# A planner's instruction times, steps of one half of the partitions, and one product moved from GpSimd to VectorE

## The chip, the cores and the metric

The kernel runs on one core of a Trainium2 chip. TensorE multiplies matrices (PE in the profile; PEld is its weight load), VectorE (DVE), ScalarE (ACT) and GpSimd (POOL) work on elements, SyncE (SP) issues transfers. The metric is the device time of one execution in microseconds; the median of three runs before the change is 2248.6 us (2247.82 to 2249.54).

## The reference

One decoder layer over 2048 tokens of width 1024, all in float32. The normalised input is projected by one wide matrix; the pieces feed three branches, whose outputs are gated, projected, merged and added to the input.

```python
h = rms_norm(x, norm_g[l])
p = h @ w_in[l]
y_a = rwkv7_mix(...) * jax.nn.silu(z_a)
y_b = sliding_window_sink_attn(...) * jax.nn.silu(z_b)
y_c = memory_cross_attn(...) * jax.nn.silu(z_c)
merged = gates[:, :, 0] * (y_a @ w_proj_a[l]) + gates[:, :, 1] * (y_b @ w_proj_b[l]) + gates[:, :, 2] * (y_c @ w_proj_c[l])
x = x + merged @ w_out[l]
```

Branch A is a recurrence over time with 8 heads of width 64. Its keys are normalised per head: `kk = kk / max(norm(kk), 1e-12)`. The change touches the place where those norms enter.

## The kernel before

**Tiling.** Tokens are worked in four blocks of 512 (`sb`), channels by 128 partitions. Large matmuls are 128x128 by 128x512 and come in threes: each float32 operand is split into a high and a low part, and `gemm3` (L457, L458, L459) adds high times high, high times low, low times high in one PSUM tile. `wblock` brings such weights: in the first block from the inputs, with the split on ScalarE (L439) and VectorE (L440) and a copy of it kept in DRAM; later from that copy.

**Streams.** In a block two streams are interleaved. `stream_r` is branch A, two groups of two head pairs. A pair occupies 128 partitions: the even head the lower 64, the odd head the upper 64 (`EV`, `OD`). `rwkv_prep` makes the operands of a pair. Within it, `dk` holds one over the squared norms (L722), and L723 and L724 fill the tile `AB` [128, 8 chunks, 128] on GpSimd: the right half with the mask `gmask`, the left half with `gmask` times `dk`, both broadcast. L726 to L737 and L742 make the operands Q and BK from the keys, decays and receptance on VectorE; 32 matmuls (L753) into four PSUM banks multiply them; L760 and L761 take the results out of PSUM, multiplying by `AB` and by `gmask`, for each bank first one half of the partitions, then the other. L770 transposes BK on TensorE; L766 and L771 copy on ScalarE. `rwkv_inverse` solves small triangular systems, mostly on VectorE (L803 to L805). `rwkv_chain` walks over the 8 chunks: two bursts of small matmuls on the state Z (L866, L867), W (L869), two more (L874, and L859 of the chunk before), a product with `dk` (L878), L881, and L882 for the next state; L872 prepares a scaled state on ScalarE. The small steps of the chain come for the even and the odd head in turn. `stream_f` has cross attention (`cross_head`), window attention (`swa_kv`, `swa_pair`), the merges of branches C and B and the gates of A. At the end of a block come the merge of A and the output projection (L1172 to L1174, L1179).

**Order.** The program is first written down as a list of instructions. `steps` turns each into a `Step` with what it reads and writes, those that it must follow, a rank (its place in the list, with shifts: steps outside TensorE that read PSUM move ahead by 600, the inverse's back by 500), and a cost by engine. `busy` is how long its engine is taken, `dur` how long until its result is there. Two steps that read the same PSUM tile are kept in the order of the list. `lay_out` then plays the program through with these costs: a clock for each engine, the time from which each step is ready, the buffers as they come free. Whenever an engine is free it takes, of the steps ready by then, the one of lowest rank; TensorE, once in a small tile of its array, stays with steps of that tile while it finds any. `order` makes the resulting sequence of every engine binding. So the costs never change what is computed, only in which order each engine does it.

Of the kernel before, what the change touches and what calls it, by code (L numbers as in the profile page):

```python
# [14 lines left out]
ALU = mybir.AluOpType  # L15
# [12 lines left out]
C = 64  # L28
NC_ = TB // C
# [26 lines left out]
class Step:  # L56


    def __init__(self, ins, masks):
        self.ins, self.eng = ins, NAMES[ins.engine]  # L60
        self.reads, self.writes = ([self.region(a.bass_ap, masks) for a in aps if getattr(a, "bass_ap", None) is not None]
                                   for aps in (ins.ins, ins.outs))
        self.reads, self.writes = ([r for r in l if r] for l in (self.reads, self.writes))
        self.before, self.after, self.opens, self.group, self.end = set(), [], [], [], None
        self.lat = LAT[self.eng]
        if self.eng == "PE" and not any(r[0].startswith(("Z_", "W_", "R_")) or r[0] in ("Z", "W", "R") for r in self.reads):
            self.lat = 600
        self.bytes = 512 * self.n((self.writes + self.reads)[0]) if self.is_dma() else 0
        getattr(self, "cost_" + ("SP" if self.bytes else self.eng))()

# [25 lines left out]
    def cost_PE(self):  # L96
        out, mov, w = self.writes[0], *self.reads[:2]
        n = self.n(out)
        self.tile = tuple(128 if r[3][0][1] > 64 else 64 if r[3][0][1] > 32 else 32 for r in (mov, out))
        self.dense = mov[5] == F32R  # L100
        if self.dense:
            self.busy = 14 + 0.424 * n
        elif self.ins.is_transpose:
            self.busy = 108 if self.tile[0] == 128 else 55
        elif self.tile[1] == 128:
            self.busy = 223 + max(0, n - 128) * 1.7 if self.tile[0] == 128 else 62 + max(0, n - 64) * 0.8
        else:
            self.busy = 32 if self.tile[1] == 32 else max(58, 0.86 * n)
        self.dur = max(270, self.busy + 160)

    def cost_ACT(self):
        r = self.reads[0]
        self.dur = (170 if r[4] else 206) + 0.83 * self.n(r) + 90 * (len(self.reads) - 1 + len(self.writes) - 1)
        self.busy = self.dur - (85 if len(self.writes) > 1 else 38 if r[4] else -12)
        self.table = {AF.Sin: 1, AF.Exp: 2, AF.Tanh: 2}.get(self.ins.func, 0)

    def cost_DVE(self):
        r, two = self.reads[0] if self.reads else self.writes[0], sum(self.n(x) > 1 for x in self.reads) > 1
        slow = two or r[4] or type(self.ins).__name__ not in ("InstTensorScalarPtr", "InstTensorCopy", "InstMemset")
        self.dur = 155 + (1.05 if slow else 0.53) * self.n(r) + 30 * (len(self.reads) - 1)  # L120
        self.busy = max(100, self.dur - 85)
        if two and r[4] and self.n(r) <= 128:
            self.busy = self.dur + 20

    def cost_POOL(self):
        n = self.n(self.writes[0])
# [54 lines left out]
def lay_out(tc, todo):  # L181

    metas = {tag: meta.bufs for p in tc.info.pools if p.space != bass.MemoryType.DRAM for tag, meta in p.tag_meta.items()}
    source = {t.name: t.source_name for t in tc.info.tiles}
    tags = {tag: Tag(b) for tag, b in metas.items()}
    users, opened = {}, set()
    for s in todo:
        for name in {r[0] for r in s.reads + s.writes}:
            users.setdefault(name, []).append(s)
        for r in s.writes:  # L190
            if source[r[0]] in tags and r[0] not in opened:
                opened.add(r[0])
                s.opens.append(r[0])
                tags[source[r[0]]].queue.append(r[0])
    left = {name: len(u) for name, u in users.items()}
    heads = {tag: 0 for tag in tags}
    clock = {e: 0.0 for e in NAMES.values()}
    ready, parked = {e: {} for e in clock}, set()
    orders = {e: [] for e in clock}
    missing = {s: len(s.before) for s in todo}  # L200

    def seen_by(s, b):

        if b.eng == s.eng:
            return 0 if s.eng == "PE" else b.end + 30
        return b.end + s.lat

    def room(s):

        at, taken = 0.0, {}  # L210
        for name in s.opens + [n for g in s.group for n in g.opens]:
            tag = source[name]
            t, i = tags[tag], taken.get(tag, 0)
            if t.queue[heads[tag] + i] != name or len(t.free) <= i:
                return None
            taken[tag] = i + 1
            old = t.free[i]
            if old:
                at = max([at] + [seen_by(s, b) for b in last[old].values()])
        return at  # L220

    def offer(s):
        at = room(s)
        if at is None:
            parked.add(s)
            ready[s.eng].pop(s, None)
        else:
            parked.discard(s)
            ready[s.eng][s] = max([at] + [seen_by(s, b) for b in s.before])

    last = {name: {} for name in users}
    for s in todo:
        if not missing[s]:
            offer(s)
    tile, fp32, wires, table = (128, 128), False, 0, 2
    for _ in todo:
        best = None
        for e, rs in ready.items():
            if rs:
                at = max(clock[e], min(rs.values()))  # L240
                if best is None or at < best[0]:
                    best = at, e
        at, e = best
        can = [s for s, t in ready[e].items() if t <= at]
        s = min(can, key=lambda s: s.rank)
        if e == "PE":
            if tile != (128, 128) and s.tile != tile:
                s = min(can, key=lambda s: (s.tile != tile, s.dense, s.rank))
            if s.tile != tile:
                at += 95  # L250
            clock[e] = at + s.busy
            if s.dense and fp32:
                clock[e] += 95
            elif s.tile != tile and s.tile[1] < 128:
                clock[e] += 49
            tile, fp32 = s.tile, not s.dense
        else:
            if e == "ACT" and not s.bytes and s.table and s.table != table:
                at, table = at + 1280, s.table
            clock[e] = at + s.busy  # L260
        s.end = at + s.dur
        if s.bytes:
            wires = s.end = max(wires, s.end) + s.bytes / 330
        del ready[e][s]
        orders[e].append(s)
        again = set()
        for name in s.opens:
            tag = source[name]
            tags[tag].free.pop(0)
            heads[tag] += 1  # L270
            again.add(tag)
        for name in {r[0] for r in s.reads + s.writes}:
            if e not in last[name] or last[name][e].end < s.end:
                last[name][e] = s
            left[name] -= 1
            if not left[name] and source[name] in tags:
                tags[source[name]].free.append(name)
                again.add(source[name])
        for a in s.after:
            missing[a] -= 1  # L280
            if not missing[a]:
                offer(a)
        if again:
            for a in [a for rs in (parked, *ready.values()) for a in rs if any(source[n] in again for g in [a, *a.group] for n in g.opens)]:
                offer(a)
    return orders
# [11 lines left out]
def build(tc, A, nsb=4):  # L298
    nc = tc.nc
    es = ExitStack()  # L300
    V, S, G, PE = nc.vector, nc.scalar, nc.gpsimd, nc.tensor
# [82 lines left out]
    gmask = cp.tile([128, 128], BF16, name="gmask")  # L384
# [286 lines left out]
    def rwkv_prep(p, i, Z, dk, Nc, sb, hT, lwla, group):  # L671
        def big(name):

            if not i:
                return rp.tile([128, NC_, 128], F32, name=name)
            t = wp.tile([128, NC_, 128], F32, name="whl")
            G.memset(t[:, 0, 0:1], 0.0)
            return t

        QE, QO, AB, BK = (big(n) for n in ("QE", "QO", "AB", "BK"))  # L680
# [40 lines left out]
                    V.tensor_scalar(own[h, :, o], sums[at, :, e], 1e-24, None, op0=ALU.max)  # L721
        V.reciprocal(dk[:, i], dk[:, i])  # L722
        G.tensor_copy(AB[:, :, C:], gmask[:, C:].unsqueeze(1).to_broadcast([128, NC_, C]))  # L723
        G.tensor_tensor(AB[:, :, :C], gmask[:, :C].unsqueeze(1).to_broadcast([128, NC_, C]), dk[:, i].unsqueeze(2).to_broadcast([128, NC_, C]), op=ALU.mult)  # L724
        kkh = tmp()
        V.tensor_scalar(kkh, k, dcol("hk_k", p), None, op0=ALU.mult)  # L726
        for Q, h in ((QE, EV), (QO, OD)):
# [12 lines left out]
        r = shift(rpj, B_R + p, pcol("mu_r", p), dcol("omu_r", p), sb, "rr_")  # L740
# [6 lines left out]
        two = ((QE, EV, OD), (QO, OD, EV))  # L747
# [631 lines left out]
```

## Time and profile before

| | |
|---|---|
| median of three runs | 2248.6 us |
| profiled execution | 2250.41 us |
| its span, first to last instruction | 2248.6 us |
| ScalarE steps / VectorE steps / GpSimd steps | 2024 / 3951 / 209 |
| VectorE's inverse, L803 + L804 + L805 | 113.3 + 104.4 + 102.9 us |
| weight split, L439 and L440 | 111.1 and 123.3 us |
| read and written in HBM | 333.24 and 94.90 MB |

A row of the groups gives line, engine, operation, output and inputs, shape, count, then busy us, mean ns of one, and the idle time of the engine before them with what ended it. Matmuls overlap in the pipe, and their ends are modelled, so their spacing is read from the starts in the timeline and not from their durations. A row of the timeline is start, length, engine, line, operation; "x4" is four merged ones.

### The profile page before, as it was taken

How to read it: one execution, taken by the hardware profiler on the slowest of the kernel's cores; microseconds unless marked ns; L12 is line 12 of the kernel's file. 1: busy time of each engine (PE TensorE's matmuls, PEld its weight loads, DVE VectorE, ACT ScalarE, POOL GpSimd, SP SyncE). 2: the span in 40 equal slices, each digit the busy share in tenths (PEclk: the TensorE clock that was granted, in tenths of full speed). 3: DMA queues.
4: the chain of work that ended last, by engine and by line, in shares of the span. 5: the costliest groups of instructions: out<-in, count | busy, mean ns of one | idle time of the engine just before them, and what ended most of it. 6: DMA issues, size and time to landing. Idle time of an engine off the chain costs nothing.

```text
span 2248.6 us, 36877 instructions
## 1 busy us (share of the span) xinstructions
PE 2219.2 (99%) x13706; PEld 1804.8 (80%) x13706; DVE 1531.7 (68%) x3951; ACT 926.1 (41%) x2024; POOL 149.7 (7%) x209
## 2 busy tenths in 40 slices
PE   8999999999999999999999999999999999999999
PEld 7887778778888778878888878787878887787887
DVE  6799699775479777953437957985245895896312
ACT  6664565545253354423214345442223435434210
POOL 2000010000000011000000001000000001100000
PEclk9999999999999999999999999999999999999999
DMA  6767556679944444447774434445675444343655
GB/s 215 271 232 245 191 188 220 221 269 353 324 146 160 134 141 150 147 165 235 239 239 136 164 122 150 148 135 195 229 250 199 157 142 160 115 148 132 206 191 193
DMA packets 146226, 430.55 MB, mean 191 GB/s; under 512 B 16640, under 2 KB 21120, under 8 KB 146048
## 3 DMA queue, kind: packets, MB, share of 16 engines
q1 hardware_dynamic: 129920, 398.83, 52.4%
q10 hardware_dynamic: 16128, 29.37, 4.0%
q8 instruction: 109, 1.79, 0.3%
q14 instruction: 69, 0.57, 0.1%
HBM read 333.24 MB, written 94.90 MB: 190 GB/s over the span
## 4 chain that ended last, share of the span: by engine, by line
PE 73%; DVE 18%; ACT 3%; DMA 2%; issue 2%; POOL 1%; SPq 0%; ACTq 0%; DVEq 0%; POOLq 0%
PE mm L457 18%; PE mm L459 18%; PE mm L458 17%; DVE ibc L803 2%; DVE ibc L804 1%; PE rw L881 1%; DVE Yi L805 1%; PE mm L1172 1%; PE mm L1173 1%; PE mm L1174 1%; ACT g L1102 1%; PE oo L1003 1%; DVE whl L440 1%; PE rw L866 1%; PE rw L874 1%
## 5 line engine op out<-in xcount | busy, mean ns | idle before, releaser
L457 PE MATMUL mm<-hH,whl 128*128 128x512 f32 x1888 | 750.0, 397 | 1.5 <-DVE gt L928 1.5
L459 PE MATMUL mm<-hH,whl 128*128 128x512 f32 x1888 | 748.3, 396 | 0.0
L458 PE MATMUL mm<-hL,whl 128*128 128x512 f32 x1888 | 748.0, 396 | 0.0
L457 PEld LDWEIGHTS mm<-hH,whl 128*128 128x128 f32 x1888 | 354.8, 188 | 72.7 <-DVE gt L928 1.9
L459 PEld LDWEIGHTS mm<-hH,whl 128*128 128x128 f32 x1888 | 354.8, 188 | 69.7
L458 PEld LDWEIGHTS mm<-hL,whl 128*128 128x128 f32 x1888 | 355.0, 188 | 67.8 <-issue 0.5
L439 ACT ACTIVATE whl<-raw 128x512 fp32r<-128x512 f32 x178 | 111.1, 629 | 144.8 <-PE mm L459 89.7
L440 DVE TENSOR_TENSOR whl<-raw,whl 128x512 fp32r<-128x512 f32 x178 | 123.3, 696 | 52.3 <-ACT whl L439 51.5
L457 PE MATMUL mm<-yh,whl 128*128 128x512 f32 x384 | 151.5, 395 | 1.4 <-DVE gt L1155 0.8
L459 PE MATMUL mm<-yh,whl 128*128 128x512 f32 x384 | 150.8, 393 | 0.0
L458 PE MATMUL mm<-yl,whl 128*128 128x512 f32 x384 | 150.7, 392 | 0.0
L872 ACT ACTIVATE SP<-Z,Pl 64x64 f32<-64x64 f32 x256 | 88.3, 345 | 112.7 <-DVE Z L882 109.2
L803 DVE STREAM_SHUFFLE ibc<-Nc 128x496 f32<-128x496 f32 (+30 forms) x248 | 113.3, 472 | 0.1
L1155 DVE SCALAR_TENSOR_TENSOR g<-g,mm 128x512 f32<-128x512 f32 x32 | 21.8, 680 | 128.6 <-PE mm L459 128.5
L804 DVE TENSOR_TENSOR ibc<-ibc,Yi 128x496 f32<-128x496 f32 (+30 forms) x248 | 104.4, 421 | 4.0
L805 DVE TENSOR_TENSOR Yi<-Yi,ibc 128x496 f32<-128x496 f32 (+30 forms) x248 | 102.9, 415 | 0.9
L1140 ACT ACTIVATE gt<-mm 128x512 f32<-128x512 f32 x64 | 38.0, 594 | 145.3 <-PE mm L459 145.1
L882 DVE SCALAR_TENSOR_TENSOR Z<-rw,Pl,SP 64x64 f32<-64x64 f32 x224 | 63.5, 283 | 50.0 <-PE rw L881 46.4
L457 PEld LDWEIGHTS mm<-yh,whl 128*128 128x128 f32 x384 | 72.1, 188 | 17.3 <-DVE g L1155 1.5
L459 PEld LDWEIGHTS mm<-yh,whl 128*128 128x128 f32 x384 | 72.1, 188 | 14.9
L458 PEld LDWEIGHTS mm<-yl,whl 128*128 128x128 f32 x384 | 72.1, 188 | 14.1
L1102 ACT ACTIVATE g<-g,mxs,st 128x256 f32<-128x256 f32 (+1 forms) x128 | 74.5, 584 | 18.8 <-DVE mxs L1095 18.6
(1812 smaller groups left out, 3786.7 us busy)
## 6 DMA issues: line engine op xcount, KB each, us to landing
whl<-k SPq DMA_DIRECT2D x486, 512.0 KB, 3.4
k<-whl SPq DMA_DIRECT2D x162, 512.0 KB, 4.3
raw<-in_w_in SPq DMA_DIRECT2D x118, 256.0 KB, 3.3
g<-in_x ACTq DMA_DIRECT2D x32, 256.0 KB, 4.4
out<-g ACTq DMA_DIRECT2D x32, 256.0 KB, 4.9
raw<-in_w_proj SPq DMA_DIRECT2D x24, 256.0 KB, 3.1
rt<-in_x ACTq DMA_DIRECT2D x24, 256.0 KB, 5.2
rt<-in_xt ACTq DMA_DIRECT2D x24, 256.0 KB, 5.8
```

The source lines that it names most:

```text
L439: S.activation(w[:, 0], raw, AF.Copy)
L440: V.tensor_tensor(w[:, 1], raw, w[:, 0].bitcast(F32), op=ALU.subtract)
L457: PE.matmul(out, lh, rh, start=i == 0, stop=False)
L458: PE.matmul(out, lh, rl, start=False, stop=False)
L459: PE.matmul(out, ll, rh, start=False, stop=i == n - 1)
L803: V.stream_shuffle(bc[:, :, :w], N_[:, :, s + 1:], [s] * 32)
L804: V.tensor_tensor(bc[:, :, :w], bc[:, :, :w], Y[:, :, s:s + 1].to_broadcast([128, n, w]), op=ALU.mult)
L805: V.tensor_tensor(Y[:, :, s + 1:], Y[:, :, s + 1:], bc[:, :, :w], op=ALU.add)
L872: S.activation(SP[h, i], Z[h, i, e, c], AF.Copy, scale=g[4][h, c:c + 1])
L882: upds = [V.scalar_tensor_tensor(Sst[h, g[0]] if c == NC_ - 1 else Z[h, i, e, c + 1], pS[h, i, e], g[4][h, c:c + 1], SP[h, i], op0=ALU.mul ...
L1102: S.activation(prs[b][:, i, m0:], prs[b][:, i, m0:], AF.Exp, scale=r2[:, b, i:i + 1], bias=mx[:, b, i:i + 1], accum_out=mx[:, b, 2 + i:3 + i])
L1140: S.activation(t, gp, AF.Tanh, scale=0.5)
```

## The change

Three edits. First, the formulas for `busy` and `dur` on TensorE, ScalarE and VectorE get other constants and cases: a scan has a fixed 1225 ns, shuffles and transposes 40 ns more, small operands are charged at 60 ns, a ScalarE step takes its engine for 97 ns less than its duration (15 with an accumulator). On TensorE a change of the tile delays the result by 97 ns and holds the engine 205 ns longer on the way back to large matmuls, 150 to other full tiles, 140 into small ones; the charge of 95 ns for a large matmul after a full-tile float32 one is gone.

Second, each step notes in `rows` the partition at which its output starts, and the highest at which an input starts. On VectorE and ScalarE the planner adds 20 to the rank of a step whose `rows` differ from those of the engine's last, and 105 ns to its start. Full-height steps and those of the lower half both start at 0, so they count as alike.

Third, the product of mask and norms (L724 before) goes from GpSimd to VectorE; the operands are the same. The term added to `seen_by` is zero for every engine.

```diff
+        outs = [a.bass_ap for l in (ins.outs, ins.ins) for a in l if getattr(a, "bass_ap", None) is not None]
+        rows = [a.offset // math.prod(list(a.tensor.shape)[1:]) for a in outs[:1] + [a.bass_ap for a in ins.ins if getattr(a, "bass_ap", None) is not None]]
+        self.rows = rows[0], max(rows)
...
-            self.busy = 14 + 0.424 * n
+            self.busy = 15 + 0.4167 * n
         elif self.ins.is_transpose:
-            self.busy = 108 if self.tile[0] == 128 else 55
+            self.busy = 112 if self.tile[0] == 128 else 55
         elif self.tile[1] == 128:
-            self.busy = 223 + max(0, n - 128) * 1.7 if self.tile[0] == 128 else 62 + max(0, n - 64) * 0.8
+            self.busy = 221 + max(0, n - 128) * 1.64 if self.tile[0] == 128 else 66 + max(0, n - 64) * 0.75
...
-        self.dur = (170 if r[4] else 206) + 0.83 * self.n(r) + 90 * (len(self.reads) - 1 + len(self.writes) - 1)
-        self.busy = self.dur - (85 if len(self.writes) > 1 else 38 if r[4] else -12)
+        self.dur = (170 if r[4] else 206) + 0.83 * self.n(r) + 90 * (len(self.reads) - 1)
+        self.busy = self.dur - (15 if len(self.writes) > 1 else 97)
...
-        self.dur = 155 + (1.05 if slow else 0.53) * self.n(r) + 30 * (len(self.reads) - 1)
-        self.busy = max(100, self.dur - 85)
-        if two and r[4] and self.n(r) <= 128:
-            self.busy = self.dur + 20
+        self.dur = 152 + (1.042 if slow else 0.52) * self.n(r) + 60 * (len(self.reads) - max(wide, 1))
+        if "Scan" in kind:
+            self.dur = 1225
+        elif kind in ("InstStreamShuffle", "InstStreamTranspose"):
+            self.dur += 40
+        self.busy = max(70, self.dur - 83)
...
-        s = min(can, key=lambda s: s.rank)
+        s = min(can, key=lambda s: s.rank + 20 * (e in ("DVE", "ACT") and s.rows != rows[e]))
...
+            clock[e] = at + s.busy
             if s.tile != tile:
-                at += 95
-            clock[e] = at + s.busy
-            if s.dense and fp32:
-                clock[e] += 95
-            elif s.tile != tile and s.tile[1] < 128:
-                clock[e] += 49
-            tile, fp32 = s.tile, not s.dense
+                at += 97
+                clock[e] += 205 if s.dense else 150 if s.tile == (128, 128) else 140
+            tile = s.tile
...
+            if s.rows != rows[e] and e in ("DVE", "ACT") and not s.bytes:
+                at += 105
+                rows[e] = s.rows
...
-        G.tensor_tensor(AB[:, :, :C], gmask[:, :C].unsqueeze(1).to_broadcast([128, NC_, C]), dk[:, i].unsqueeze(2).to_broadcast([128, NC_, C]), op=ALU.mult)
+        V.tensor_tensor(AB[:, :, :C], gmask[:, :C].unsqueeze(1).to_broadcast([128, NC_, C]), dk[:, i].unsqueeze(2).to_broadcast([128, NC_, C]), op=ALU.mult)
```

More of the change, by code (lines that the diff above doesn't have):

```diff
@@ L101, in cost_PE @@
         if self.dense:
-            self.busy = 14 + 0.424 * n
+            self.busy = 15 + 0.4167 * n
         elif self.ins.is_transpose:
-            self.busy = 108 if self.tile[0] == 128 else 55
+            self.busy = 112 if self.tile[0] == 128 else 55
         elif self.tile[1] == 128:
-            self.busy = 223 + max(0, n - 128) * 1.7 if self.tile[0] == 128 else 62 + max(0, n - 64) * 0.8
+            self.busy = 221 + max(0, n - 128) * 1.64 if self.tile[0] == 128 else 66 + max(0, n - 64) * 0.75
         else:
-            self.busy = 32 if self.tile[1] == 32 else max(58, 0.86 * n)
+            self.busy = 32 if self.tile[1] == 32 else max(60, 0.88 * n)
         self.dur = max(270, self.busy + 160)
@@ L112, in cost_ACT @@
         r = self.reads[0]
-        self.dur = (170 if r[4] else 206) + 0.83 * self.n(r) + 90 * (len(self.reads) - 1 + len(self.writes) - 1)
-        self.busy = self.dur - (85 if len(self.writes) > 1 else 38 if r[4] else -12)
+        self.dur = (170 if r[4] else 206) + 0.83 * self.n(r) + 90 * (len(self.reads) - 1)
+        self.busy = self.dur - (15 if len(self.writes) > 1 else 97)
         self.table = {AF.Sin: 1, AF.Exp: 2, AF.Tanh: 2}.get(self.ins.func, 0)
     def cost_DVE(self):
-        r, two = self.reads[0] if self.reads else self.writes[0], sum(self.n(x) > 1 for x in self.reads) > 1
-        slow = two or r[4] or type(self.ins).__name__ not in ("InstTensorScalarPtr", "InstTensorCopy", "InstMemset")
-        self.dur = 155 + (1.05 if slow else 0.53) * self.n(r) + 30 * (len(self.reads) - 1)
-        self.busy = max(100, self.dur - 85)
-        if two and r[4] and self.n(r) <= 128:
-            self.busy = self.dur + 20
+        r, wide = self.reads[0] if self.reads else self.writes[0], sum(self.n(x) > 1 for x in self.reads)
+        kind = type(self.ins).__name__
+        slow = wide > 1 or r[4] or kind not in ("InstTensorScalarPtr", "InstTensorCopy", "InstMemset")
+        self.dur = 152 + (1.042 if slow else 0.52) * self.n(r) + 60 * (len(self.reads) - max(wide, 1))
[4 more added lines that the diff above has]
+        self.busy = max(70, self.dur - 83)
     def cost_POOL(self):
@@ L205, in seen_by @@
             return 0 if s.eng == "PE" else b.end + 30
-        return b.end + s.lat
+        return b.end + s.lat + (0 if s.eng == "PE" else 0)
     def room(s):
@@ L234, in lay_out @@
             offer(s)
-    tile, fp32, wires, table = (128, 128), False, 0, 2
+    tile, wires, table = (128, 128), 0, 2
+    rows = {e: (0, 0) for e in clock}
     for _ in todo:
```

## The prediction

> **What bounds the kernel now.** I read the page's busy times first, then the busy time by stretches of the span, then the chain of waits of TensorE alone, and last the timeline around its waits.
>
> ```profile
> span 2248.6 us, 36877 instructions
> PE 2219.2 (99%) x13706; PEld 1804.8 (80%) x13706; DVE 1531.7 (68%) x3951; ACT 926.1 (41%) x2024; POOL 149.7 (7%) x209
> ```
>
> TensorE is busy for all but 29.4 us of 2248.6. Nothing in the change removes a matmul, so there are two places to win or lose: those 29.4 us, and time inside the busy figure that is not matmul work. The stretches show where the idle time lies (columns: stretch, length, busy us of PE, weight loads, DVE, ACT, POOL, clock, DMA share, GB/s).
>
> ```profile
> 0.00:25.00 25.00, 18.49 (x76) 15.66 (x77) 15.98 (x52) 13.03 (x30) 5.21 (x17) 0.80 0.70 226
> 25.00:500.00 475.00, 465.26 (x3090) 377.40 (x3090) 399.41 (x1004) 271.42 (x586) 43.00 (x55) 1.00 0.66 228
> 500.00:1025.00 525.00, 522.32 (x3271) 424.73 (x3270) 372.83 (x967) 220.69 (x482) 34.80 (x47) 1.00 0.56 192
> 1025.00:1087.00 62.00, 62.00 (x275) 51.35 (x274) 16.01 (x29) 16.96 (x34) 1.21 (x2) 1.00 0.68 227
> 1087.00:2181.00 1094.00, 1087.21 (x6721) 883.08 (x6719) 706.07 (x1869) 398.96 (x887) 65.46 (x88) 1.00 0.52 172
> 2181.00:2249.00 68.00, 63.97 (x283) 52.64 (x281) 21.42 (x32) 5.06 (x8) 0.00 (x0) 1.00 0.57 192
> ```
>
> Idle is 6.5 us in the first 25 (inputs arriving) and 4.0 at the end (last adds and stores, minus 0.4 of rounding of the window). Neither is a matter of order alone. Between lie 9.7 in the first block, 2.7, 0.0 and 6.8: 19.2 us. That is all that a better order can take out of idle time. The fourth row matters for the rivals: for 62 us before a block's last merge TensorE has work that waits for nobody, so the recurrent chain may end that much later at no cost. The waits behind the 19.2 us, from 25 us on (who waited, for whom, sum, times, longest):
>
> ```profile
> PE rw L866 <- DVE Z L882: 2.3, 4, 1.4
> PE rw L770 <- DVE QE L761: 2.1, 3, 0.7
> PE rw L753 <- DVE whl L737: 1.8, 1, 1.8
> PE mm L457 <- DVE gt L928: 1.5, 1, 1.5
> PE rw L770 <- DVE whl L761: 1.3, 3, 0.5
> PE rw L881 <- DVE Z L878: 1.3, 4, 0.4
> PE oo L1128 <- ACT g L1120: 1.0, 3, 0.4
> PE rw L785 <- DVE carry L661: 1.0, 3, 0.4
> PE rw L753 <- DVE QO L742: 0.8, 1, 0.8
> ```
>
> Nearly all end with VectorE, though VectorE is busy only 68%. The order on each engine is fixed when the program is built, by a planner that picks a step once it believes its inputs are there. With other matmuls in plenty, such a wait means that the planner had the VectorE step earlier, or TensorE later, than the chip did. So the question is which durations it had wrong, and whether the change mends those.
>
> **The change part by part.** *Product of mask and norms, GpSimd to VectorE.* 16 steps, two per group of two pairs.
>
> ```profile
> L724 POOL TENSOR_TENSOR AB<-gmask,dk 128x512 f32<-128x512 bf16 x8 | 11.5, 1436 | 52.7 <-DVE dk L722 52.7
> L724 POOL TENSOR_TENSOR whl<-gmask,dk 128x512 f32<-128x512 bf16 x8 | 10.9, 1358 | 185.2 <-DVE dk L722 185.2
> L732 DVE TENSOR_TENSOR BK<-rt x16: 674/690/1532, 68.5 to 1921.2; 64x512 f32<-64x512 f32 x16
> L732 DVE TENSOR_TENSOR whl<-rt x16: 629/686/1445, 117.8 to 1963.8; 64x512 f32<-64x512 f32 x16
> 826.14 0.64 DVE L735 TENSOR_TENSOR rk__8671<-rk__8671,rt 128x512 f32<-128x512 f32 x1
> 826.30 1.38 POOL L724 TENSOR_TENSOR AB<-gmask,dk 128x512 f32<-128x512 bf16 x1 [1.77 <-DVE dk L722]
> 826.69 1.53 DVE L732 TENSOR_TENSOR BK<-rt 64x512 f32<-64x512 f32 x1
> 828.15 0.68 DVE L742 TENSOR_TENSOR QE<-rr__8782,Pt 64x512 f32<-64x512 f32 x1
> ```
>
> The step leaves GpSimd at 1.36 to 1.44 us and lands on VectorE at about 0.69 (the median of L732, the same kind and size; two-operand steps start 0.60 to 0.70 apart, below). That is 16 x 0.6 to 0.7 = 9.6 to 11.2 us of VectorE added. But while GpSimd works on L724, from 826.30, the VectorE step beside it takes 1.53 instead of 0.69: 0.84 lost, and L732's longest in the other row is as long. If each of the 16 costs its neighbour 0.84 the move gives back 13.4 us; taking the lower bound, that only the two longest rows of L732 show it, 1.6 us. VectorE's sum changes by -3.8 to +9.6; I take about zero, because the timeline shows the loss where I looked. Nothing queues behind L724 on GpSimd for long: it is 7% busy. What gains is the plan: the old one had no 0.84 in it, and the steps after it (L737, L742, L760, L761) are those that L753 and L770 wait for. Four of the waits above, 2.1 + 1.3 + 1.8 + 0.8 = 6.0 us, lie behind such steps.
>
> [...]
>
> *Half of the partitions.* On VectorE a change between steps at partition 0 and at 64 shows in the starts:
>
> ```profile
> 837.32 0.68 DVE L761 TENSOR_TENSOR QO<-rw,gmask 64x512 f32<-64x512 f32 x1
> 837.93 0.67 DVE L760 TENSOR_TENSOR AB<-yps,AB 64x512 f32<-64x512 f32 x1
> 838.63 0.69 DVE L760 TENSOR_TENSOR AB<-oo,AB 64x512 f32<-64x512 f32 x1
> 839.25 0.69 DVE L761 TENSOR_TENSOR QE<-yps,gmask 64x512 f32<-64x512 f32 x1
> 839.95 0.69 DVE L761 TENSOR_TENSOR QO<-oo,gmask 64x512 f32<-64x512 f32 x1
> ```
>
> By the code QO and the yps AB write partitions 0 to 63, the oo AB and QE the upper half. Same half: 0.61 and 0.62 from start to start; change: 0.70 and 0.70. So a change costs 0.08 to 0.09; the old formula gives 155 + 538 + 30 - 85 = 638 ns for each, the new one 603, or 708 with its 105. Grouping these eight steps saves two or three changes, 0.2 us a pair, 16 x 0.2 = 3.2 us of VectorE. It does less than its name: steps that read one PSUM tile keep the program's order in the planner, so L882's four, which alternate, stay as they are. On time I cost the saving at zero: TensorE's work covers it, and if that cover were gone it would be worth the 3.2.
>
> *Durations.* Rows for the two largest corrections:
>
> ```profile
> L697 DVE TENSOR_TENSOR_SCAN rt<-smask,rt 128x512 f32<-128x512 bf16 x16 | 19.6, 1224 | 0.5
> L457 PE MATMUL mm<-hH,whl 128*128 128x512 f32 x1888 | 750.0, 397 | 1.5 <-DVE gt L928 1.5
> L457 PE MATMUL mm<-yh,whl 128*128 128x512 f32 x384 | 151.5, 395 | 1.4 <-DVE gt L1155 0.8 <-DVE g L1155 0.6
> 789.36 0.50 PE L458 MATMUL mm<-hL,whl 128*128 128x512 f32 x1
> 789.70 0.40 PE L459 MATMUL mm<-hH,whl 128*128 128x512 f32 x1
> 790.02 0.33 PE L874 MATMUL rw<-W,AB 64*64 64x64 f32 x4
> 790.63 0.50 PE L457 MATMUL mm<-hH,whl 128*128 128x512 f32 x1
> 790.97 0.39 PE L458 MATMUL mm<-hL,whl 128*128 128x512 f32 x1
> 791.20 0.40 PE L459 MATMUL mm<-hH,whl 128*128 128x512 f32 x1
> ```
>
> The scan takes 1224 ns; the old plan had 722, the new 1225. Large matmuls start 0.23 us apart (790.97 to 791.20), planned before at 14 + 0.424 x 512 = 231 ns, now 228. Over (1888 + 384) x 3 = 6816 of them that is 6816 x 2.7 ns = 18 us of plan by which TensorE was held to be slower than now. A TensorE that runs ahead of its plan arrives at VectorE's results too early, which is the sign of the waits above. A break into small tiles costs 0.09 going in (0.32 against 0.23), about 0.11 on the second large matmul after it (0.34), and something between: I call it 0.3. The plan's sum for a round trip hardly moves (95 + 49 + 95 + 95 = 334 before, 140 + 205 = 345 after). ScalarE's corrections change a queue that is 41% busy; only L1128's 1.0 us above is behind it.
>
> **The sum.** I count as removed the waits behind misjudged steps: 6.0 us (L770, L753), and in the recurrent chain L866's 2.3 and L881's 1.3, where small steps and the 0.1 of a half change decide: 9.6 us. L457, L785, L1128 and the rest I leave, since a new order has errors of its own. The profiled execution took 2250.4 us, 1.8 more than its span and than the median of the runs shown, 2248.6. So 2250.4 - 9.6 = 2240.8 for such an execution, and 2239.0 for the median. Bounds: all 19.2 removed gives 2229.4; none, 2248.6.
>
> **Rivals.** A difference under 0.2%, 4.5 us, is no difference here.
>
> *The waits move.* Of the 19.2 us the rows above hold 12.1, and the rest lies in smaller waits; a new order may lose these and find as many elsewhere. For it: most last 0.4 to 0.8 us, about one VectorE step. Against: the corrections have one sign. Half the gain kept or none: 2244 to 2253.
>
> *Fewer breaks.* By the code L866, L874 and L881 come in 64 bursts each (8 chunks, 2 groups, 4 blocks), 192 breaks. If accurate times let a fifth of them join others, 38 x 0.3 = 11.5 us go as well: 2239.0 - 11.5 = 2227.5. Against: which tile TensorE prefers is unchanged.
>
> *More breaks (the other side).* With 20 places of penalty, an upper-half step is passed by ready full-height ones, since these share the lower half's key. At L760 and L761 the second PSUM bank is then freed up to three steps, 1.9 us, later, so L770's transposes fall apart from other small work. The chain's delay is covered by the 62 us; the extra breaks are not covered. A fifth more of them costs 11.5 us: 2248.6 + 11.5 = 2260.1 with the waits unchanged. It decides from about 47 extra breaks on, where 0.3 x 47 = 14.1 exceeds the gain of 9.6 by 4.5; below that it only eats the gain.
>
> *VectorE late in the first block.* There it works 399 of 475 us, and L724 now stands ahead of L728 and L732 by rank. If none of the 0.84 comes back, 16 x 0.69 = 11.0 us on the path: 2259.6. Against: the freed neighbour stands in the same place.
>
> [...]
>
> **Chances and range.** Forecast 0.45 (own range 2229 to 2244), fewer breaks 0.10, waits move 0.19, more breaks 0.17, VectorE late 0.09. Faster 0.45 + 0.10 = 0.55; same 0.19; slower 0.26. The range 2223 to 2261 holds the forecast, the fewer breaks and the middle, and the slower cases up to their prices; about 2 in 10 is left outside.
>
> **What would show it.** Right: L732's longest near 0.70, GpSimd below 130 us (149.7 - 22.4), TensorE's waits for L761 and L737 gone, its idle total near 20 us. More breaks: TensorE's busy time above 2219 with idle time unchanged. VectorE late: more wait for L737 and L742 before 500 us. The prediction is wrong if idle time stays at 29 us, or if it falls and the busy time grows by as much.

## The result, and the profile after

| | before | changed |
|---|---|---|
| median of six runs | 2248.36 us | 2235.34 us |
| ratio, 95% interval | | 0.9939 [0.9928, 0.9951] |
| profiled execution, its span | 2250.41, 2248.6 us | 2234.0, 2232.2 us |

The change makes the kernel 0.6% faster. The two profiled executions are 16.4 us apart, the medians only 13.0: the execution before lies 2.1 us above its median, the changed one 1.3 below. The page of the changed kernel, and its busy time by the same stretches and with the same columns as in the prediction (all lines of the code stand 7 lower now):

```profile
span 2232.2 us, 36875 instructions
PE 2213.4 (99%) x13706; PEld 1803.3 (81%) x13706; DVE 1524.9 (68%) x3967; ACT 909.3 (41%) x2024; POOL 132.0 (6%) x193
```

```profile
0.00:25.00 25.00, 19.07 (x110) 16.80 (x111) 17.88 (x59) 16.28 (x38) 6.62 (x19) 0.93 0.73 237
25.00:500.00 475.00, 468.32 (x3083) 380.00 (x3083) 397.69 (x1007) 265.12 (x581) 36.61 (x50) 1.00 0.67 231
500.00:1025.00 525.00, 524.10 (x3281) 426.45 (x3280) 376.13 (x980) 215.99 (x482) 30.21 (x43) 1.00 0.56 193
1025.00:1087.00 62.00, 62.00 (x277) 51.35 (x276) 12.70 (x24) 18.52 (x36) 1.21 (x2) 1.00 0.66 227
1087.00:2181.00 1094.00, 1092.27 (x6754) 889.87 (x6754) 710.35 (x1888) 391.58 (x888) 57.35 (x80) 1.00 0.51 173
```

TensorE executes the same 13706 matmuls. The span is 16.4 us shorter: its idle time fell from 29.4 to 18.8 us (10.6), its busy time from 2219.2 to 2213.4 (5.8). Between 25 and 2181 us the idle time is now 6.7 + 0.9 + 0.0 + 1.7 = 9.3 us, where it was 19.2. What it still waits for from 25 us on (the first rows of its chain of waits):

```profile
PE as__2655 L1093 <- DVE mxs L1097: 1.8, 1, 1.8
PE rw L777 <- ACT BK L778: 1.4, 1, 1.4
PE rw L786 <- ACT rt L784: 0.7, 1, 0.7
PE rw L917 <- DVE rt L914: 0.6, 1, 0.6
PE oo L644 <- DVE whl L447: 0.6, 2, 0.3
PE as__16831 L1179 <- DVE g L1186: 0.6, 1, 0.6
PE rw L873 <- DVE Z L889: 0.4, 1, 0.4
```

The waits of the transposes (now L777) for L768 and of the pair products (L760) for L744 and L749 are gone; of the chain's, L873 keeps 0.4 of 2.3 us. The transposes wait once for ScalarE instead, 1.4 us at L778, which is new. The neighbour of the moved product, now L739, and the product itself on VectorE, with shortest, median and longest in ns:

```profile
L739 DVE TENSOR_TENSOR BK<-rt x16: 672/680/690, 66.0 to 1907.4; 64x512 f32<-64x512 f32 x16
L739 DVE TENSOR_TENSOR whl<-rt x16: 672/677/692, 111.8 to 1950.1; 64x512 f32<-64x512 f32 x16
L731 DVE TENSOR_TENSOR AB<-gmask,dk x8: 672/682/693, 73.1 to 1904.9; 128x512 f32<-128x512 bf16 x8
L731 DVE TENSOR_TENSOR whl<-gmask,dk x8: 676/693/694, 120.8 to 1951.4; 128x512 f32<-128x512 bf16 x8
```

No step of L739 is long any more: the longest was 1532 ns and is 692.

**Where the busy time went.** A matmul's end in the trace is modelled, so a part of each wait can hide in busy time. In the run without the halves (below) the timeline of TensorE has this:

```profile
837.70 0.40 PE L462 MATMUL mm<-hL,whl 128*128 128x512 f32 x1
837.94 0.39 PE L463 MATMUL mm<-hH,whl 128*128 128x512 f32 x1
839.33 0.63 PE L774 MATMUL rw<-c_ident,BK 128*128 128x128 f32 x4 [1.00 <-DVE QO L765]
```

L774 starts 1.39 us after L463, where 0.24 is the spacing of the rows above it: 1.15 lost, of which 1.00 counts as idle. This wait hides 0.15 us, and at that figure a wait shorter than 0.15 us would not be seen at all. From 25 us on, the waits over 50 ns number 45 before and 27 after, counted in the two traces. If each hides as much, that is 18 x 0.15 = 2.7 of the 5.8 us.

A second part is the granted clock in these two executions. Two neighbouring matmuls of one shape in each, before and then after, and the stretches in which half the clock was granted, one before and two after (columns as above, the clock third from the end):

```profile
22.14 0.41 PE L458 MATMUL mm<-mB,whl 128*128 128x256 f32 x1
22.36 0.41 PE L459 MATMUL mm<-mB,whl 128*128 128x256 f32 x1
24.21 0.28 PE L465 MATMUL mm<-mB,whl 128*128 128x256 f32 x1
24.33 0.28 PE L466 MATMUL mm<-mB,whl 128*128 128x256 f32 x1
14.30:24.50 10.20, 8.59 (x40) 8.03 (x39) 9.23 (x25) 5.58 (x14) 2.66 (x5) 0.50 0.51 151
12.40:15.70 3.30, 3.30 (x17) 3.06 (x16) 3.16 (x11) 2.13 (x7) 0.95 (x2) 0.50 0.92 294
309.40:312.70 3.30, 3.30 (x14) 2.55 (x12) 3.27 (x14) 2.69 (x7) 0.00 (x0) 0.50 0.62 235
```

Such matmuls start 0.22 us apart at half the clock and 0.12 at the full one. TensorE works 8.6 us at half the clock before and 6.6 after, which is some 1.0 us of busy time less. The first 22 matmuls, in a stretch for which the clock has records only in part, took 7.66 us before and 6.74 after, 0.9 less. So about 2 of the 5.8 us are clock, and not waits. In the medians the clock counts for less: the mean granted clock was 0.998 or 0.999 in all six executions of the changed kernel, and averages 0.998 in those of the kernel before that stand beside the experiments.

Breaks into small tiles, counted in the traces, are 181 before and 179 after, worth 0.6 us at the prediction's estimate of 0.3 each. What is left of the 5.8 would be shorter waits; the trace does not divide it.

### The profile page after: what moved, and what is told of

Read it like the earlier page. It is cut to its first block, busy times and chain, and to the rows that moved or that the text cites. A ratio compares the mean times of both kernels' runs of the same rounds, so it can differ in the third digit from the quotient of the medians.

```text
span 2232.2 us, 36875 instructions
## 1 busy us (share of the span) xinstructions
PE 2213.4 (99%) x13706; PEld 1803.3 (81%) x13706; DVE 1524.9 (68%) x3967; ACT 909.3 (41%) x2024; POOL 132.0 (6%) x193
## 4 chain that ended last, share of the span: by engine, by line
PE 63%; DVE 19%; ACT 3%; issue 1%; DMA 1%; POOL 1%; ACTq 0%; DVEq 0%; SPq 0%; POOLq 0%
PE mm L464 15%; PE mm L466 15%; PE mm L465 15%; DVE ibc L810 2%; DVE ibc L811 1%; PE mm L1179 1%; PE mm L1181 1%; PE mm L1180 1%; PE rw L888 1%; DVE Yi L812 1%; DVE g L1097 1%; PE rw L873 1%; PE oo L1010 1%; DVE whl L447 1%; PE rw L881 1%
## 5 line engine op out<-in xcount | busy, mean ns | idle before, releaser
L879 ACT ACTIVATE SP<-Z,Pl 64x64 f32<-64x64 f32 x256 | 76.8, 337 | 113.0 <-DVE Z L889 111.3
```

The costliest lines, as they stand in the source:

```text
L879: S.activation(SP[h, i], Z[h, i, e, c], AF.Copy, scale=g[4][h, c:c + 1])
```

## The experiments

All times are medians; each group of runs has its own runs of the kernel before on the same chip, so the ratios are compared.

### The move alone

```diff
-        G.tensor_tensor(AB[:, :, :C], ...
+        V.tensor_tensor(AB[:, :, :C], ...
```

> The kernel before with one edit: the product of mask and norms on VectorE instead of GpSimd; all costs of the planner as before. Theory (waits behind misjudged steps): the 0.5 to 0.9 us that a VectorE step loses beside each of the 16 GpSimd products goes, and with it most of the 6.0 us that TensorE waits at the small matmuls of the pair products and at the transposes of BK: 4 to 6 us faster, 2242 to 2244. Rival 1 (the whole 13 us are the move): 2235. Rival 2 (the gain is the luck of a new order): anything from 2235 to 2255, with waits in new places. Rival 3 (the move only adds VectorE work): 2250 or more.

Measured: 2239.60 against 2248.96 us, ratio 0.9958 [0.9945, 0.9970], 9.4 us faster: more than the 4 to 6 of the theory, and some two thirds of the whole. The page, and the first waits of TensorE:

```profile
PE 2214.6 (99%) x13706; PEld 1806.5 (81%) x13706; DVE 1530.8 (68%) x3967; ACT 929.5 (42%) x2026; POOL 129.7 (6%) x193
```

```profile
PE mm L457 <- DVE gt L928: 2.6, 1, 2.6
PE rw L866 <- DVE Z L882: 1.4, 4, 0.6
PE rw L910 <- DVE rt L907: 1.4, 2, 0.7
PE rw L881 <- DVE Z L878: 1.1, 3, 0.4
...
PE rw L770 <- DVE whl L761: 0.5, 1, 0.5
```

VectorE executes 16 more steps and is busy 1530.8 us where it was 1531.7: what it took over and what it no longer loses beside GpSimd cancel. The trace of the kernel before shows this for every product: beside each of the 16 on GpSimd, one VectorE step is 0.54 to 0.87 us longer than the median of its line and shape, 11.4 us in all, and 16 steps of 0.69 are 11.0. TensorE's idle time falls by 6.7 us, from 29.4 to 22.7, about what the theory had; its busy time falls by 4.6 as well. L770's wait falls from 2.1 + 1.3 to 0.5 us and L753's is gone. The chain's waits are smaller but still there.

### The change without the move

```diff
-        V.tensor_tensor(AB[:, :, :C], ...
+        G.tensor_tensor(AB[:, :, :C], ...
```

> The changed kernel with the product back on GpSimd; the new costs and the grouping by halves stay. Theory: the loss beside GpSimd is back and is in no cost of the planner, so waits of TensorE at the pair products and the BK transposes come back: 2239 to 2241, idle time of TensorE 4 to 6 us above the changed kernel's 18.8. Rival 1 (the whole gain is the move): 2248. Rival 3: 2235 or less, since VectorE has 10 us less to do.

Measured: 2243.69 against 2248.96 us, 0.9977 [0.9967, 0.9988]. All that is not the move is worth 0.23%, and with the move 0.61%. The loss is larger than the theory's: idle time is 26.9 us, 8.1 above the changed kernel's where 4 to 6 were expected. The longest of L739 is back at 1526 and 1535 ns, and TensorE waits again where the theory had it:

```profile
L739 DVE TENSOR_TENSOR BK<-rt x16: 674/689/1526, 67.8 to 1916.5; 64x512 f32<-64x512 f32 x16
L739 DVE TENSOR_TENSOR whl<-rt x16: 672/684/1535, 114.5 to 1958.9; 64x512 f32<-64x512 f32 x16
```

```profile
PE rw L777 <- DVE QE L768: 2.2, 1, 2.2
PE rw L760 <- DVE QO L749: 2.0, 3, 0.7
PE rw L777 <- DVE whl L768: 1.8, 4, 0.5
```

### The TensorE costs: alone, and undone

The edit is the part of the diff in `cost_PE` and the charges for a change of the tile, put on the kernel before, and taken back in the changed kernel.

> The kernel before with the new TensorE costs alone (matmul times and the charges for a change of the tile). Theory: the old plan had TensorE 2.7 ns too slow for each large matmul and 95 ns for each large one after a full-tile float32 one, so TensorE came early to results of the other engines; with this mended 4 to 7 us faster, 2241 to 2245, and the waits at the BK transposes stay, since the loss beside GpSimd is not mended. Rival (the costs of VectorE and ScalarE carry it): within 2 us of before.

Measured: 2245.19 against 2248.96 us, 0.9983 [0.9974, 0.9992]: 3.8 us, just short of the 4 to 7 expected.

> The changed kernel with the old TensorE costs; the new VectorE and ScalarE costs, the halves and the move stay. Theory: half of the gain is lost, 2239 to 2243, with waits of TensorE spread over many places. Rival (the costs of VectorE and ScalarE and the move carry it): 2236 or less.

Measured: 2239.61 against 2248.96 us, 0.9955 [0.9943, 0.9968]. The interval overlaps that of the change, so the loss of about 4 us is likely and not certain. The page has TensorE busy 2219.0 us, and its span is 2235.5: idle is only 16.5 us, less than in the changed kernel, but 5.6 us of busy time are back. Breaks into small tiles number 186 there, 7 more than in the changed kernel, an estimated 2.1 us at 0.3 each; where the rest of the 5.6 comes from stays open. It is not the clock, which was higher in this run (0.999 to 1.0 in its five executions).

### The old durations of VectorE and ScalarE

The changed kernel with `cost_ACT` and `cost_DVE` of before and without the second edit.

> The changed kernel with the old durations of VectorE and ScalarE and without the halves: only the new TensorE costs and the move are left of the change. If the parts add up, the move (9.4 us) and the TensorE costs (3.8 us) already make the whole of it: 2235 to 2237, and the new durations of VectorE and ScalarE, halves included, are worth nothing by themselves. Theory (waits behind misjudged VectorE steps are a part of their own): 2238 to 2241, TensorE's idle time 3 us or more above the changed kernel's.

Measured: 2239.59 against 2249.54 us, 0.9961 [0.9948, 0.9973], the same as the move alone. By the medians, the 3.8 us of the TensorE costs are not there on top of the move. But the granted clock was lower in these five executions, 0.995 to 0.997 with a mean of 0.9964, where the move alone has a mean of 0.9976 and the change 0.9982. Matmuls of one shape start 0.22 us apart at half the clock and 0.12 at the full one (above), nearly twice, so each 0.001 is an estimated 2.2 us at most of a span of 2235: 2.7 us against the move alone and 4.0 against the change, which is nearly all of the 4.3 us between the medians. The trace speaks for the theory all the same: idle time is 24.1 us, 5.3 above the changed kernel's, where 3 or more were expected. Whether the parts add up, and what the new durations of VectorE and ScalarE bring by themselves, is not settled by these runs.

### Without the halves, and with parts of them

```diff
-        s = min(can, key=lambda s: s.rank + 20 * (e in ("DVE", "ACT") and s.rows != rows[e]))
+        s = min(can, key=lambda s: s.rank)
...
-            if s.rows != rows[e] and e in ("DVE", "ACT") and not s.bytes:
-                at += 105
-                rows[e] = s.rows
```

> The changed kernel without its second edit: neither the 20 places of penalty nor the 105 ns for a change of the half; the new durations and the move stay. Theory: the grouping saves VectorE little and TensorE covers it, but the 105 ns are part of the true durations, so 1 to 3 us slower than the changed kernel, 2236 to 2239. Rival (the grouping carries the gain): 2242 or more. Rival (more breaks, from upper halves put off): faster than the changed kernel, below 2233.

Measured: 2265.57 against 2248.57 us, 1.0074 [1.0061, 1.0086]: 17 us slower than before, 30 slower than the change. No theory had said that. TensorE's page row and its first waits:

```profile
span 2263.1 us, 36858 instructions
...
PE 2229.4 (99%) x13706; PEld 1799.5 (80%) x13706; DVE 1530.0 (68%) x3967; ACT 926.4 (41%) x2024; POOL 131.4 (6%) x193
```

```profile
PE rw L774 <- DVE whl L765: 2.8, 4, 1.4
PE rw L789 <- DVE carry L665: 2.2, 3, 0.7
PE rw L774 <- DVE QO L765: 2.2, 3, 1.0
```

Lines stand 4 lower here than before the change. The transposes (L774) and the wait for `carry` (L789) are places that waited before the change too, and wait longer; idle is 33.7 us. The busy time is 10.2 us above that of the kernel before. There are 64 waits over 50 ns from 25 us on, 19 more, which would hide 2.9 of it; breaks into small tiles are 182, so the rest is not theirs, and it stays open. The next run has the penalty of 20 places taken away, the first of the three lines above, and the 105 ns left in.

> The changed kernel without the 20 places of penalty, but with the 105 ns for a change of the half. Theory: within 2 us of the changed kernel, 2233 to 2238; if the run without both is slower and this one is not, it is the duration that counts and not the grouping. Rival (the grouping counts): as slow as without both.

Measured: 2233.92 against 2248.57 us, 0.9936 [0.9922, 0.9949], the same as the change. So the grouping itself is worth nothing that can be measured, though it does what it says on ScalarE. There the four steps that scale the state (L879) are in pairs in the changed kernel and alternate without the penalty; one row of each, in this order:

```profile
788.86 1.18 ACT L879 ACTIVATE SP<-Z,Pl 64x64 f32<-64x64 f32 x4
```

```profile
792.98 1.42 ACT L879 ACTIVATE SP<-Z,Pl 64x64 f32<-64x64 f32 x4
```

Two changes of the half less save 0.24 us for the four, and ScalarE's busy time is 909.3 us with the penalty and 926.8 without. TensorE covers it. What counts is the 105 ns as a duration. The trace of this run also warns of reading single waits: with the move in place, the transposes wait once for L768, 1.9 us, and the pair products once for L749, 1.5 us, and the run is as fast as the change. The next run has both parts of the edit on VectorE alone (`e in ("DVE",)` in both lines).

> The changed kernel with the penalty and the 105 ns for a change of the half on VectorE alone, none on ScalarE. Theory (VectorE is what TensorE waits for): within 3 us of the changed kernel, 2233 to 2239. Rival (the loss without halves came from ScalarE, whose steps are then planned 105 ns too short at every change): 2245 or more.

Measured: 2244.94 against 2249.54 us, 0.9980 [0.9972, 0.9989]: some 9 us slower than the change and outside the theory's 2233 to 2239. So ScalarE's halves matter too, though it is 41% busy; of the two parts taken from it, the penalty was worth nothing in the run before, which leaves the 105 ns. The last of these has no halves at all, but longer VectorE steps.

```diff
-        self.busy = max(70, self.dur - 83)
+        self.busy = max(70, self.dur - 45)
```

> The changed kernel without the halves, as the run that was 30 us slower, but with 38 ns more on every VectorE step, so that a 512-element step is planned at 641 ns, between the 603 and 708 of the two cases and near the old 638. Theory (what cost the 30 us is that the plan had VectorE too fast on the whole): most of it comes back, 2236 to 2244. Rival (the plan must know which steps change the half): 2252 or more.

Measured: 2245.22 against 2249.54 us, 0.9984 [0.9975, 0.9993]. Most of the loss is recovered, a little less than expected, by a flat 38 ns that knows nothing of halves, and the result equals the run with halves on VectorE alone. In both, ScalarE is planned without the 105 ns at each change, where the rows above have 0.12 us. Of the 1.0074 - 0.9939 = 1.35%, then, 0.9% goes with VectorE planned too fast on the whole, and the remaining 0.45% with ScalarE; that this remainder is ScalarE's alone is argued from the equality of the two runs, and a flat correction on both was not tried. The equality is also a rough one: the mean granted clock was 0.9963 with the flat correction and 0.9975 with halves on VectorE, an estimated 2.7 us.

### Is it the luck of an order?

```diff
-LAT = {"PE": 200, "DVE": 45, "ACT": 35, "POOL": 80, "SP": 30}
+LAT = {"PE": 200, "DVE": 50, "ACT": 35, "POOL": 80, "SP": 30}
```

> The kernel before with one planner constant that stands for no measured thing moved a little: the latency after a VectorE step from 45 to 50 ns. It gives another order of the same work, with the same kinds of error in the plan. Theory: within 3 us of before, 2246 to 2252, VectorE again losing some 12 us beside GpSimd, and TensorE's idle time near 29 us. Rival (the gain is the luck of a new order): 5 us or more off, to either side.

Measured, on the kernel before: 2247.15 against 2248.57 us, 0.9992 [0.9983, 1.0001].

> The changed kernel with the same shift of the latency from 45 to 50 ns. Theory: within 3 us of the changed kernel, 2233 to 2239. Rival (luck): back towards 2245.

Measured, on the changed kernel: 2233.21 against 2248.57 us, 0.9934 [0.9922, 0.9947]. Another order from the same costs moves neither kernel by more than about 2 us. Two draws are few, but the gain of 13 us is not of that size.

### The two variants that came out lowest, together

> The changed kernel without the 20 places of penalty and with 50 ns of latency after a VectorE step, the two variants that came out a little below the changed kernel, together. Theory (both are within the scatter of orders): 2231 to 2237. Rival (both are real): 2229 to 2232.

Measured: 2234.96 against 2249.54 us, 0.9935 [0.9923, 0.9948]. No better than either, as expected if both were scatter, and no version here is measurably faster than the changed kernel.

## Why the prediction was right

The time predicted was 2239.0, the time measured 2235.34; the direction, the main cause and most of the size were right.

**Idle time.** 9.6 us of waits were counted as removed, and between 25 and 2181 us 9.9 are gone. Of the rows counted, about 0.5 us are left. The other waits were 9.6 us and are 8.8, largely in new places. The wait behind the product is the best-supported term: undoing the move brings back L739's long steps, the waits of L777 and L760, and 8.5 us. That the move leaves VectorE's sum where it was, which I chose from one neighbour in the timeline, is right to a microsecond (1531.7 to 1530.8 in the move alone); one neighbour was thin evidence, but the 11.4 us lost beside the 16 products bear it out.

**The mis-sized term.** I gave the move 6.0 us; alone it is worth 9.4, and the change without it loses 0.38% (0.9977 against 0.9939), 8.5 us. The 6.0 were the waits named in the list, and as idle time they were about right: 6.7 us went in the move alone. The forecast had no term for busy time, which fell by 4.6 us in the move alone and by 5.8 with the whole change. Waits hidden in it account for an estimated 2.7 of the 5.8, and about 2 are the clock of the two executions compared.

**TensorE's costs.** The 18 us by which the old plan had it too slow were offered as the reason for the waits. The spacing is as the new plan has it: from 40 us on, large matmuls with nothing between them start 227 ns apart in both traces (median), planned at 231 before and 228 now. But the 18 us are not worth that much: 3.8 us alone, likely about as much when undone in the changed kernel, and on top of the move alone nothing that these runs can tell from the clock. A plan with a slow TensorE may be late everywhere by the same share, on which an order hardly depends; that is an explanation and was not tested.

**The halves.** That grouping costs or saves nothing on time was right (0.9936 without the penalty). But I priced the second edit as grouping only. Its 105 ns belong to the new durations: 603 ns is right for a step that follows one of the same half (0.61 and 0.62 us in the prediction's rows), and is 0.1 us short for one that does not (0.70), where the old 638 lay between. With the new base and without the 105 the plan is worse than the old one, by 17 us against the kernel before.

**ScalarE.** "A queue that is 41% busy" was the wrong ground to pass over its costs: planned too fast, it costs 9 us. Its busy share did not tell how exactly its results had to be foreseen.

**Rivals.** More breaks and fewer breaks: neither happened, with 181 breaks into small tiles before and 179 after, where the prediction had worked out 192 from the code and asked for a fifth more or less. VectorE late in the first block: no, the wait for L744 is gone there. The waits move: in part, as L1093's 1.8 us, L777's 1.4 for ScalarE and L786's 0.7 are new. The rows that the prediction showed for this hold 13.1 of the 19.2 us and not 12.1; nothing else is worked out from that. GpSimd's busy time is 132.0 us, not below 130 as I had worked out; its other steps got a little longer, 132.0 us in all where they were 127.3.

What stays open: which ScalarE steps make the 9 us, what the TensorE costs and the new durations are worth on top of the move, and where the busy time of the slow orders comes from.

## What to carry to other kernels

Where a fixed order comes from a planner, a wait of the bounding engine names a step that the plan had too early: look for what lengthens the steps in front of it, and above all for what no cost in the plan can express, as here the product on GpSimd beside which a VectorE step took 0.54 to 0.87 us longer. When the durations of a plan are replaced by measured ones, the conditions under which they were measured go with them; half of such a correction can be worse than none. Before one believes a gain of a few tenths of a per cent from a new order, a shift of a constant that means nothing shows how far orders scatter, and the granted clock of the executions shows whether the two were run at the same speed (its means lie between 0.9963 and 0.9992 in these runs).

## What the runs showed of the hardware that was not expected

A change between the halves of the partitions costs time on ScalarE as well: four 64x64 steps take 1.42 us when they alternate and 1.18 in pairs, 0.12 us for each of the two changes saved. On VectorE the prediction's rows show such a cost: a step starts 0.61 or 0.62 us after the one before it in the same half, 0.07 ahead of that one's end, and 0.70 us after it, 0.01 to 0.03 behind its end, where the half changes. For ScalarE the rows of L879, without the penalty and with it, show it.

The granted clock went with the order of the instructions: its mean was 0.9992 in five executions with the old TensorE costs and 0.9964 in five with the old durations of VectorE and ScalarE, with no overlap between the two, while the same matmuls ran. By the estimate above that is 6 us, as much as some of the parts compared here. What in an order sets it, no run here shows.
